# Layer 1 feed-forward entry: high parts of the first weights moved to ScalarE's gaps, modulation per channel tile, block sums on VectorE, one written order

## The chip, the cores and the metric

The kernel runs on one core of a Trainium2 chip. The metric is the device time of one execution in microseconds; three runs of the kernel before give a median of 1838.54 us (1838.1 to 1839.96). The engines are called by the names of the profile: PE is TensorE's matmuls, PEld its weight loads, DVE is VectorE, ACT is ScalarE, POOL is GpSimd, SP is SyncE, which here only issues transfers.

## The reference

The reference is one step of a two-layer trunk on 128 context tokens and 512 latent tokens of width 1024: layer 0 mixes tokens by differential attention, layer 1 by a bidirectional gated recurrence, and each layer ends with a dense SwiGLU feed-forward network. What matters here is where layer 1 enters its feed-forward network:

```python
def adanorm(x, g, shift, scale):
    return rmsnorm(x, g) * (1.0 + scale) + shift

def swiglu(h, w_in, w_out):
    gt, up = jnp.split(h @ w_in, 2, axis=-1)
    return (jax.nn.silu(gt) * up) @ w_out
...
        xs = xs + ms[2] * os_
        xs = xs + ms[5] * swiglu(adanorm(xs, g_norm_ffn[i], ms[3], ms[4]), w_ffn_in[i], w_ffn_out[i])
```

The hidden width is 2816. All inputs are fp32.

## The kernel before, in words

**Precision by parts.** Each operand of a product is split into a high part (an fp32r copy made by ACT) and a low part (source minus high part, made by DVE or POOL). A product is three matmuls: high by high, high by low, low by high. So nothing can be multiplied before an ACT copy and a subtraction have been made of it.

**Tokens and tiles.** The 640 tokens are five row tiles of 128 (t = 0 is the context). They are also two halves of 320, and the width of 1024 is eight channel tiles of 128 (k = 0 to 7). `Hf` holds the modulated activations in fp32, channels on partitions; `A1hi`/`A1lo` are the parts of the first half of the tokens, `A2hi`/`A2lo` and `S[:, 3]` those of the second half. `S` reuses the two tiles that held the attention-side operand `oT`, so it shows as `Thi`/`Tlo` in the profile.

**Entry to the feed-forward network, row tile by row tile.** The last product of the token mixer (`row_sums(t)`, 24 matmuls of 512 columns into `psr`) gives a row tile's second half. `close_rows(t)` adds it to the residual (two DVE steps), squares and sums it (ACT), makes the reciprocal root (three small POOL steps) and scales the rows (ACT) into an `xr` tile. `turn_rows(t)` transposes these rows on PE, eight blocks of 128 by 128, into two PSUM tiles `ntp` of four channel tiles each; there are only two such buffers, so the next row tile's transposes wait until this one's have been read. `modulate(t)` reads them: two DVE multiplications of 512 columns by the scale, broadcast along the tokens, and two additions of the shift, on POOL for t = 0, 1, 3 and on DVE for t = 2, 4. Then `hi_of` (ACT) and `lo_of` (DVE) make the parts.

**The first two hidden tiles, f = 0 and 1,** are multiplied in the plain way by `whole_in(ch, half)`: 48 matmuls of 320 columns each, SiLU on ACT and a product on DVE. Their weights `w0`, `w1` are two raw tiles each (`wr`, three buffers), split by `split_raw` (ACT 1024 columns, DVE 1024 columns) into `wh`, `wl` (six buffers each).

**From f = 2 on** `ffn_in` uses a seven-product block scheme (Strassen's with Winograd's sums) over the two halves of channels and tokens. It needs sums of activation blocks, made once by `sums(t)` for t = 2, 3, 4 (each two POOL steps, two DVE steps and the parts of three of the four results; the fourth, `s4`, is split by `put_late_sums`), and sums of weight blocks for each f, made by POOL in `ffn_weights(f)` (four steps) and split by ACT and DVE. The products are taken in the order 1, 2, 6, 5, 7, 3, 4; product 6 is added onto the PSUM tile of product 1 after ACT has copied it out.

**What sets the order.** A planner orders each engine's queue by its own cost estimates, with two exceptions. While `traced["order"]` is true, DVE, ACT and POOL instructions keep the order in which the code lists them; while `pe["strict"]` is true, the matmuls do. Weight loads on SP's queue (`load`) keep their order among themselves throughout. In the kernel before, both flags are cleared after `ffn_weights(2)`, ahead of the second `whole_in`. An instruction at the head of an engine's queue that waits holds up everything behind it.

## Time and profile before

| | |
|---|---|
| median of three runs | 1838.54 us (1838.1 to 1839.96) |
| profiled execution: time, span | 1841.69 us, 1839.9 us |
| PE busy | 1778.1 us, 97% of the span |
| DVE, ACT, POOL busy | 1219.6, 742.6, 663.8 us |
| stage of the change | about 1345 to 1445 us of the span |
| mean granted TensorE clock | 0.99 |

The profile comes from one execution, with its own time; the time lies 1.8 us above the span. Views by line all show line 51 for DVE, ACT and POOL and lines 96 and 99 for matmuls and transposes, since helpers record every operation, so instructions are told apart by the tiles that they write and read. A row of the timeline gives the start, the length, engine, line, operation, tiles, shape and count, and in brackets the idle time ahead of it and what ended it. "PEclk" is the granted clock as a share of full speed.

### The profile page before, as it was taken

The numbers are of one execution on the slowest core, as the hardware profiler recorded it, in microseconds if no ns is written. First come the engines' busy times: TensorE is split into PE (matmuls) and PEld (weight loads), VectorE is DVE, ScalarE is ACT, GpSimd is POOL, SyncE is SP. The second block draws the span as 40 slices with busy tenths as digits, with TensorE's granted clock in tenths as the row PEclk, the third lists the DMA queues.
The fourth block names the chain that finished last, engine by engine and source line by source line (L and its number), as shares of the span: only waits on it lengthen the run. The fifth ranks groups of instructions, "written<-read, shape, count | busy, mean of one in ns | idle before, by whom it ended". The sixth has DMA issues, their size and how long they took to land.

```text
span 1839.9 us, 34696 instructions
## 1 busy us (share of the span) xinstructions
PE 1778.1 (97%) x13791; PEld 1634.0 (89%) x13791; DVE 1219.6 (66%) x2092; ACT 742.6 (40%) x1642; POOL 663.8 (36%) x766
## 2 busy tenths in 40 slices
PE   6999999999999999999999999999998999999997
PEld 5799999878898999899799999999777898998896
DVE  4788888756266655855776777666658656566666
ACT  3566666635131122132353333333344443433443
POOL 3344544325000000000055455555324466466562
PEclk9999999999999999999999999999999999999999
DMA  9511221554364433453532222221222323233331
GB/s 316 175 44 44 64 66 38 167 183 121 92 200 136 148 115 121 154 145 115 155 118 64 65 65 62 62 64 65 70 89 65 102 87 114 81 98 109 92 104 69
DMA packets 222856, 195.27 MB, mean 106 GB/s; under 512 B 10276, under 2 KB 176606, under 8 KB 222694
## 3 DMA queue, kind: packets, MB, share of 16 engines
q1 hardware_dynamic: 221888, 192.46, 33.7%
q8 instruction: 108, 1.77, 0.4%
q10 hardware_dynamic: 806, 0.60, 0.1%
q14 instruction: 54, 0.44, 0.1%
HBM read 185.64 MB, written 7.37 MB: 105 GB/s over the span
## 4 chain that ended last, share of the span: by engine, by line
PE 82%; DVE 8%; DMA 4%; ACT 2%; issue 2%; POOL 2%; SPq 0%; POOLq 0%; ACTq 0%; DVEq 0%
PE psgu L96 22%; PE psr L96 19%; PE psqkv L96 8%; PE psf L96 8%; PE psvg L96 5%; PE psu L96 4%; PE pso L96 2%; PE S L96 2%; PE psg L96 2%; PE pa L96 2%; PE po L96 1%; DMA wr<-w_ada 1%; DVE Q L51 1%; PE ptp L99 1%; DVE wl L51 1%
## 5 line engine op out<-in xcount | busy, mean ns | idle before, releaser
L51 ACT ACTIVATE wh<-wr 128x1024 fp32r<-128x1024 f32 (+2 forms) x224 | 217.2, 976 | 385.1 <-DMA wr<-w_ffn_in 111.3
L51 DVE TENSOR_TENSOR wl<-wr,wh 128x1024 fp32r<-128x1024 f32 (+2 forms) x148 | 183.0, 1240 | 198.4 <-ACT wh L51 197.2
L96 PE MATMUL psgu<-Thi,wh 128*128 128x320 f32 x880 | 272.5, 311 | 2.7 <-ACT wh L51 2.6
L96 PE MATMUL psgu<-Tlo,wh 128*128 128x320 f32 x880 | 272.2, 309 | 1.2 <-DVE Tlo L51 1.2
L51 POOL TENSOR_TENSOR wl<-wr,wh 128x341 fp32r<-128x341 f32 (+2 forms) x228 | 212.5, 962 | 166.0 <-ACT wh L51 165.4
L96 PE MATMUL psgu<-Thi,wl 128*128 128x320 f32 x880 | 271.4, 310 | 0.9 <-DVE wl L51 0.9
L51 POOL TENSOR_TENSOR nss<-nss 128x1 f32<-128x1 f32 x24 | 7.5, 312 | 454.0 <-ACT xr L51 438.0
L96 PEld LDWEIGHTS psgu<-Thi,wh 128*128 128x128 f32 x880 | 165.5, 188 | 5.4 <-ACT wh L51 3.5
L96 PEld LDWEIGHTS psgu<-Tlo,wh 128*128 128x128 f32 x880 | 165.6, 188 | 2.3 <-DVE Tlo L51 1.4
L96 PEld LDWEIGHTS psgu<-Thi,wl 128*128 128x128 f32 x880 | 165.3, 188 | 2.3 <-DVE wl L51 1.8
L96 PE MATMUL psr<-wh,Thi 128*128 128x512 f32 x380 | 153.3, 405 | 0.5 <-ACT Thi L51 0.5
L96 PE MATMUL psr<-wh,Tlo 128*128 128x512 f32 x380 | 149.0, 392 | 0.0
L96 PE MATMUL psr<-wl,Thi 128*128 128x512 f32 x380 | 148.9, 392 | 0.0
L96 PE MATMUL psr<-wh,gT 128*128 128x512 f32 (+1 forms) x448 | 140.4, 388 | 1.0 <-DVE gT L51 0.6
L96 PE MATMUL psf<-Thi,wh 128*128 128x320 f32 x384 | 123.1, 321 | 0.0
L51 DVE SCALAR_TENSOR_TENSOR acc<-wr,cT,acc 128x512 f32<-128x512 f32 x168 | 116.1, 744 | 6.6 <-DMA wr<-w_ada 6.6
L96 PE MATMUL psf<-Thi,wl 128*128 128x320 f32 x384 | 118.5, 308 | 0.0
L96 PE MATMUL psf<-Tlo,wh 128*128 128x320 f32 x384 | 118.4, 308 | 0.0
L96 PE MATMUL psqkv<-wh,Thi 128*128 128x384 f32 x320 | 109.8, 359 | 1.0 <-ACT Thi L51 1.0
L96 PE MATMUL psqkv<-wh,Tlo 128*128 128x384 f32 x320 | 105.9, 345 | 0.5 <-DVE Tlo L51 0.5
L96 PE MATMUL psqkv<-wl,Thi 128*128 128x384 f32 x320 | 104.5, 342 | 0.0
L51 DVE TENSOR_TENSOR rtmp<-psr,gate 128x512 f32<-128x512 f32 (+1 forms) x101 | 66.2, 678 | 55.2 <-PE psr L96 45.9
(289 smaller groups left out, 4695.7 us busy)
## 6 DMA issues: line engine op xcount, KB each, us to landing
wr<-w_ffn_in SPq DMA_DIRECT2D x176, 256.0 KB
wr<-w_ada SPq DMA_DIRECT2D x72, 512.0 KB
wr<-w_ffn_out SPq DMA_DIRECT2D x40, 512.0 KB
wr<-w_in_rec SPq DMA_DIRECT2D x64, 256.0 KB
wr<-w_qkv_attn SPq DMA_DIRECT2D x64, 192.0 KB
ar<-w_ada SPq DMA_DIRECT2D x24, 512.0 KB
gate<-gdram SPq DMA_DIRECT2D x28, 256.0 KB
wr<-w_o_attn SPq DMA_DIRECT2D x8, 512.0 KB
```

The lines of the kernel that those rows point to most:

```text
L51: ins = op(*a, **k)
L96: in_order(nc.tensor.matmul(*a, **k))
L99: in_order(nc.tensor.transpose(*a, **k))
```

## The change

The change touches only layer 1's `out_and_ffn_1`.

1. **Modulation.** `modulate(t)` becomes eight DVE instructions of 128 columns, one per channel tile. Each multiplies by the scale and adds the shift in one step, both taken as one value per partition. The POOL and DVE additions go.
2. **High parts of `w0` and `w1`.** `split_raw` is taken apart into `whole_hi` (ACT) and `whole_lo` (DVE). The high parts of `w0` come right after `modulate(0)`; those of `w1` come in `close_rows(3)` between the sums of squares and the scaling of the rows (`hi_next`). The low parts follow after `modulate(1)` and after `modulate(3)`. The raw load of `w1` is listed right after `modulate(0)`, that of f = 2 (`raw2`) after `close_rows(4)`.
3. **Sums.** All four steps of `sums(t)` run on DVE; their parts become `put_sums(t)`, listed later. The weight sums of f = 2 run on DVE instead of POOL; those of later f stay on POOL.
4. **Order.** `turn_rows(3)` and `modulate(3)` move ahead of the low parts of row tile 2. The sums of row tiles 2, 3 and 4 are spread over the four `whole_in` calls, which are all listed ahead of the point where both flags are cleared: f = 0 and f = 1 on the first half of the tokens, then both on the second half. The four `put_gT` follow after `put_late_sums`, still in written order.

The diff, cut to its core:

```diff
-            def modulate(t, eng):
+            def modulate(t):
                 g = 0 if t == 0 else 1
-                has = [Hf[:, ks, t * P : (t + 1) * P] for ks in HALVES]
-                a, b = ([adaC[:, l, w, g, ks].unsqueeze(2).to_broadcast([P, 4, P]) for ks in HALVES] for w in (3, 2))
-                for ha, tp, c in zip(has, turned.pop(t), a):
-                    VE.tensor_tensor(ha, tp, c, ALU.mult)
-                for ha, c in zip(has, b):
-                    eng.tensor_tensor(ha, ha, c, ALU.add)
+                tps = turned.pop(t)
+                for k in range(KT):
+                    a, b = (adaC[:, l, w, g, k : k + 1] for w in (3, 2))
+                    VE.tensor_scalar(Hf[:, k, t * P : (t + 1) * P], tps[k // 4][:, k % 4], a, b, ALU.mult, ALU.add)
...
-                PO.tensor_tensor(a22, a21, a22, ALU.add)
+                VE.tensor_tensor(a22, a21, a22, ALU.add)
                 VE.tensor_tensor(a21, a11, a21, ALU.subtract)
                 VE.tensor_tensor(a11, a22, a11, ALU.subtract)
-                PO.tensor_tensor(s4, a12, a11, ALU.subtract)
+                VE.tensor_tensor(s4, a12, a11, ALU.subtract)
+                late_sums.append((c0, c1, s4))
+
+            def put_sums(t):
+                c0, c1 = max(t * P - HTOK, 0), (t + 1) * P - HTOK
                 split_rows([v[:, :, c0:c1] for v in S31], Hf[:, :, HTOK + c0 : HTOK + c1])
-                split_rows([v[:, 2, :, c0:c1] for v in S], a11)
-                late_sums.append((c0, c1, s4))
+                split_rows([v[:, 2, :, c0:c1] for v in S], Hf[:, 0:4, c0:c1])
...
+            def ffn_weights(f):
+                raw = raw_weights(f)
+                return all_weights(*plain_weights(raw), *weight_sums(raw, PO))
...
-            def close_rows(t, ps, xc, blocks=()):
+            def close_rows(t, ps, xc, between=lambda: None):
...
-                hi_of(blocks)
+                between()
                 unit_scale(sq, xs[t], xr[t])
...
+            def whole_hi(r):
+                hi = wp.tile([P, 1024], F32R, name="wh", tag="wh", bufs=6)
+                lo = wp.tile([P, 1024], F32R, name="wl", tag="wl", bufs=6)
+                AC.activation(hi, r, AF.Copy)
+                return r, hi, lo
+
+            def whole_lo(r, hi, lo):
+                VE.tensor_tensor(lo, r, hi, ALU.subtract)
+                return hi, lo
...
-            modulate(0, PO)
+            modulate(0)
+            w0 = [whole_hi(r) for r in w0]
+            w1 = whole_weights(1)
...
-            close_rows(2, ps2, xc, early_blocks(0))
+            close_rows(2, ps2, xc, lambda: hi_of(early_blocks(0)))
             xc = load_xc(3)
-            modulate(1, PO)
-            first[0].append(split_raw(w0[0], VE))
+            modulate(1)
+            hi_of(early_blocks(1))
+            first = [[whole_lo(*w) for w in w0]]
             lo_of(early_blocks(0))
-            hi_of(early_blocks(1))
             ps3, products = row_sums(3)
             drain(products)
-            close_rows(3, ps3, xc)
+
+            def hi_next():
+                w1[:] = [whole_hi(r) for r in w1]
+
+            close_rows(3, ps3, xc, hi_next)
             xc = load_xc(4)
-            first[0].append(split_raw(w0[1], VE))
-            w1 = whole_weights(1)
             lo_of(early_blocks(1))
             ps4, products = row_sums(4)
             take(products, 2)
             turn_rows(2)
-            modulate(2, VE)
+            modulate(2)
             hi_of(early_blocks(2))
             lo_of(early_blocks(2))
             drain(products)
-            close_rows(4, ps4, xc, late_blocks(2))
+            close_rows(4, ps4, xc, lambda: hi_of(late_blocks(2)))
+            raw2 = raw_weights(WHOLE)
+            turn_rows(3)
+            modulate(3)
             lo_of(late_blocks(2))
+            hi_of(late_blocks(3))
+            first.append([whole_lo(*w) for w in w1])
+            lo_of(late_blocks(3))
...
-                    turn_rows(3)
-                    modulate(3, PO)
-                    first.append([split_raw(w, VE) for w in w1])
-                    hi_of(late_blocks(3))
-                    lo_of(late_blocks(3))
+                    sums(2)
                     gus = [whole_in(first[0], 0)]
                     turn_rows(4)
-                    modulate(4, VE)
+                    modulate(4)
                     hi_of(late_blocks(4))
+                    put_sums(2)
                     lo_of(late_blocks(4))
-                    for t in range(2, NT):
-                        sums(t)
-                    weights = ffn_weights(WHOLE)
+                    sums(3)
+                    gus.append(whole_in(first[1], 0))
+                    put_sums(3)
+                    sums(4)
+                    h1, h2 = plain_weights(raw2)
+                    gus.append(whole_in(first[0], 1))
+                    put_sums(4)
+                    weights = all_weights(h1, h2, *weight_sums(raw2, VE))
+                    gus.append(whole_in(first[1], 1))
+                    open_group(nk)
+                    put_late_sums()
+                    for i, gu in enumerate(gus):
+                        put_gT(group, i % 2, i // 2, gu)
                     traced["order"] = False
                     pe["strict"] = False
-                    gus.append(whole_in(first[1], 0))
-                    open_group(nk)
-                    for f, gu in enumerate(gus):
-                        put_gT(group, f, 0, gu)
-                    for f in range(WHOLE):
-                        put_gT(group, f, 1, whole_in(first[f], 1))
```

`raw_weights`, `plain_weights`, `weight_sums` and `all_weights` are the four parts of the old `ffn_weights`, with the engine of the sums as an argument.

More of the change, by code (lines that the diff above doesn't have):

```diff
@@ L1626, in put_gT, with raw_weights, plain_weights, weight_sums @@
                 VE.tensor_tensor(gT[1][:, i, hs], v, gT[0][:, i, hs], ALU.subtract)
-            def ffn_weights(f):
+            def raw_weights(f):
                 cols = slice(f * P, (f + 1) * P)
-                r1, r2 = (load_raw(wi[:, 4 * c : 4 * c + 4, :, cols], [4, 2, P]) for c in range(2))
-                x1, x2 = (r.rearrange("p (k u c) -> p k u c", k=4, u=2) for r in (r1, r2))
-                b11, b12, b21, b22 = x1[:, :, 0], x1[:, :, 1], x2[:, :, 0], x2[:, :, 1]
-                h1 = split(b11, VE, [4, P])
-                h2 = split(x2, VE, [4, 2, P])
-                ta, tb = (xr_tile().rearrange("p (s k c) -> p s k c", s=2, k=4) for _ in range(2))
-                PO.tensor_tensor(ta[:, 0], b12, b11, ALU.subtract)
-                PO.tensor_tensor(ta[:, 1], b22, b12, ALU.subtract)
-                PO.tensor_tensor(tb[:, 0], b22, ta[:, 0], ALU.subtract)
-                PO.tensor_tensor(tb[:, 1], b21, tb[:, 0], ALU.subtract)
+                raw = [load_raw(wi[:, 4 * c : 4 * c + 4, :, cols], [4, 2, P]) for c in range(2)]
+                return [r.rearrange("p (k u c) -> p k u c", k=4, u=2) for r in raw]
+            def plain_weights(raw):
+                x1, x2 = raw
+                return split(x1[:, :, 0], VE, [4, P]), split(x2, VE, [4, 2, P])
+            def weight_sums(raw, eng):
+                b11, b12, b21, b22 = (x[:, :, u] for x in raw for u in range(2))
+                ta, tb = (xr_tile().rearrange("p (s k c) -> p s k c", s=2, k=4) for _ in range(2))
+                eng.tensor_tensor(ta[:, 0], b12, b11, ALU.subtract)
+                eng.tensor_tensor(ta[:, 1], b22, b12, ALU.subtract)
+                eng.tensor_tensor(tb[:, 0], b22, ta[:, 0], ALU.subtract)
+                eng.tensor_tensor(tb[:, 1], b21, tb[:, 0], ALU.subtract)
+                return ta, tb
+            def all_weights(h1, h2, ta, tb):
                 tb, ta = (
@@ L1661, in out_and_ffn_1, with ffn_in @@
             }
-            def ffn_in(f, w, group, i, between=lambda: None):
+            def ffn_in(w, group, i):
                 def product(ps, n, start):
@@ L1687, in ffn_in @@
                 AC.activation(b, sum1, AF.Copy)
-                between()
                 sum2 = mm_tile([P, HTOK], "psu")
@@ L1741, in whole_weights @@
                 return [load_raw(wi[:, 4 * c : 4 * c + 4, :, f * P : (f + 1) * P], [4, 2, P]) for c in range(2)]
+            def whole_hi(r):
[6 more added lines that the diff above has]
+                return hi, lo
             traced["order"] = True
             w0 = whole_weights(0)
-            first = [[]]
             for t in range(2):
@@ L1819, in out_and_ffn_1 @@
                 for f in range(max(f0, WHOLE), f1):
-                    if f == WHOLE:
-                        ffn_in(f, weights, group, f - f0, put_late_sums)
-                    else:
-                        ffn_in(f, ffn_weights(f), group, f - f0)
+                    ffn_in(weights if f == WHOLE else ffn_weights(f), group, f - f0)
                 gT = group["gT"]
```

## The prediction

> **What bounds the kernel now.** I read the busy times of the page first, then a table of stretches, then who waited for whom on PE, then the timelines of the engines around the waits. The first row is the whole span; the second is the sum row of a table over 1440 to 1840 us (width, then busy us).
>
> ```profile
> PE 1778.1 (97%) x13791; PEld 1634.0 (89%) x13791; DVE 1219.6 (66%) x2092; ACT 742.6 (40%) x1642; POOL 663.8 (36%) x766
> ...
> sum 400.00, PE 387.52 PEld 358.33 DVE 245.92 ACT 157.76 POOL 221.72; mean PE 32.29 PEld 29.86 DVE 20.49 ACT 13.15 POOL 18.48
> ```
>
> PE sets the time, and after 1440 us it is busy for 387.5 of 400 us, most of the rest being the last 15 us of stores. So time that PE wins at the feed-forward entry should travel to the end. The entry itself, by stretches (width; busy us of PE, PEld, DVE, ACT, POOL; granted clock; DMA share; GB/s):
>
> ```profile
> 1366.00:1381.00 15.00, 14.30 (x70) 11.21 (x68) 7.50 (x12) 8.91 (x19) 5.91 (x10) 1.00 0.12 36
> 1381.00:1396.00 15.00, 10.37 (x59) 10.20 (x60) 10.70 (x17) 8.39 (x16) 4.00 (x6) 0.77 0.12 37
> 1396.00:1418.00 22.00, 22.00 (x153) 21.85 (x151) 21.16 (x25) 10.21 (x18) 11.08 (x7) 1.00 0.25 73
> 1418.00:1430.00 12.00, 4.13 (x24) 3.50 (x24) 11.01 (x12) 4.60 (x10) 7.01 (x5) 0.90 0.29 87
> 1430.00:1434.20 4.20, 4.20 (x17) 4.20 (x18) 4.20 (x5) 2.21 (x5) 3.81 (x2) 0.50 0.04 14
> ...
> PE psu L96 <- ACT wh L51: 7.0, 1, 7.0
> PE ntp L99 <- DVE Hf L51: 5.3, 2, 5.1
> PE psgu L96 <- DVE wl L51: 0.6, 1, 0.6
> ```
>
> The last three rows are PE's waits from 1366 to 1435 us (total, times, longest). There are two holes, A at 1381 and B at 1418, and behind each the clock is down. PE's timeline at their edges, and a row of the chain of waits for twelve matmuls of 320 columns at full clock:
>
> ```profile
> 1380.14 0.40 PE L96 MATMUL psr<-wh,Tlo 128*128 128x512 f32 x1
> 1385.63 1.94 PE L99 MATMUL ntp<-ident,xr 128*128 128x128 f32 x8 [5.09 <-DVE Hf L51]
> 1387.22 0.61 PE L96 MATMUL psgu<-A1hi,wh 128*128 128x320 f32 x1
> ...
> 1389.97 0.31 PE L96 MATMUL psgu<-A1hi,wh 128*128 128x320 f32 x1
> ...
> 1418.74 0.42 PE L96 MATMUL psgu<-A1hi,wl 128*128 128x320 f32 x1 [0.62 <-DVE wl L51]
> ...
> 1420.97 0.42 PE L96 MATMUL psg<-A1hi,wl 128*128 128x320 f32 x1 [0.21 <-DVE wl L51]
> ...
> 1422.40 0.31 PE L96 MATMUL psg<-A1hi,wl 128*128 128x320 f32 x1
> 1429.74 0.64 PE L96 MATMUL psu<-Thi,wh 128*128 128x320 f32 x1 [7.03 <-ACT wh L51]
> ...
> 1434.17 0.39 PE L96 MATMUL psu<-Thi,wl 128*128 128x320 f32 x1
> ...
> 1443.58 1.76 PE psgu L96 x12
> ```
>
> One matmul is 1.76 / 12 = 0.147 us. Hole A loses 5.1 us idle. Then eight transposes take 1.59 us from start to start instead of about 0.8, and nine matmuls 2.75 us (1387.22 to 1389.97) instead of 1.3: 2.2 us to the low clock. Hole B loses, start to start, 7.34 - 0.15 = 7.2 us, about 1.2 us in the two short waits ahead of it, and 4.43 - 17 x 0.147 = 1.9 us to the low clock. Sum: 5.1 + 2.2 + 1.2 + 7.2 + 1.9 = **17.6 us**, the most that the change can win here.
>
> Why the holes are there:
>
> ```profile
> 1381.39 1.04 ACT L51 ACTIVATE wh<-wr 128x1024 fp32r<-128x1024 f32 x1
> ...
> 1382.46 1.22 DVE L51 TENSOR_TENSOR wl<-wr,wh 128x1024 fp32r<-128x1024 f32 x1 [4.28 <-ACT wh L51]
> 1384.81 1.28 DVE L51 TENSOR_TENSOR Hf<-ntp,adaC 128x512 f32<-128x512 f32 x2
> ...
> 1407.72 3.76 DVE L51 TENSOR_TENSOR Tlo<-Hf,Thi 128x1024 fp32r<-128x1024 f32 x2 [0.40 <-ACT Thi L51]
> ...
> 1420.84 4.51 DVE L51 TENSOR_TENSOR gT<-gu,gT 128x320 fp32r<-128x320 f32 x3
> ...
> 1427.70 1.99 ACT L51 ACTIVATE wh<-xr 128x1024 fp32r<-128x1024 f32 x2
> ...
> 1428.78 2.36 DVE L51 TENSOR_TENSOR wl<-xr,wh 128x1024 fp32r<-128x1024 f32 x2 [0.46 <-ACT wh L51]
> ...
> L51 POOL TENSOR_TENSOR xr<-wr 128x512 f32<-128x512 f32 x4 | 7.8, 1951 | 0.0
> ```
>
> A: DVE stands 4.28 us at the low part of the second `w0` tile, whose high part ACT makes only at 1381.39, after the rows of tile 3 are scaled. Queued behind it is the modulation of row tile 2 (1384.81), which must free the PSUM tiles for the transposes of row tile 3. B: DVE works without a break from 1396 on and puts `gT` parts ahead of what product 6 needs; the split of the weight sums starts on ACT at 1427.70. POOL, working alongside, makes DVE slower: two subtractions of 1024 columns take 3.76 us at 1407.72 and 2.36 us at 1428.78, and three of 320 columns take 4.51 us.
>
> **The change part by part.**
>
> *Modulation.* No row shows a two-scalar step out of PSUM. The nearest (form, count, durations in ns; for the second busy us and mean ns; then timeline rows):
>
> ```profile
> L51 DVE TENSOR_SCALAR F<-sg,omlb,lb x32: 437/454/1052, 942.1 to 1282.8; 128x320 f32<-128x320 f32 x32
> ...
> L51 DVE TENSOR_SCALAR orow<-o,rc,rs 128x128 f32<-128x128 f32 x40 | 14.2, 356 | 2.3 <-POOL rs L51 2.2
> ...
> 1347.74 1.39 DVE L51 SCALAR_TENSOR_TENSOR orow<-po,rs,gt 128x128 f32<-128x128 f32 x5 [4.99 <-POOL rs L51]
> ...
> 1365.92 1.28 DVE L51 TENSOR_TENSOR Hf<-ntp,adaC 128x512 f32<-128x512 f32 x2
> 1366.75 1.23 PE L99 MATMUL ntp<-ident,xr 128*128 128x128 f32 x8 [0.24 <-DVE Hf L51]
> ...
> L51 DVE TENSOR_TENSOR Hf<-ntp,adaC 128x512 f32<-128x512 f32 x10 | 6.4, 679 | 0.0
> ```
>
> Low bound: one scalar and a PSUM source, five in 1.39 us, about 0.26 us from start to start. High: with two scalars out of SBUF, 320 columns take 0.437 and 128 take about 0.34, so 0.5 ns per column and 0.27 us fixed; at the 1 ns per column of the 512-column rows (two in 1.28, one 0.68, so 0.60 each) a PSUM source gives 0.27 + 0.13 = 0.40 us. Instructions overlap by some 0.08 us (0.68 against 0.60), so I take **0.32 us** each, nearest to the second row, 2.6 us per row tile, with 0.26 and 0.40 as bounds. On DVE that replaces 1.2 us (t = 0, 1, 3) or 2.4 us (t = 2, 4).
>
> The Trainium skill, "VectorE: DVE Perf Modes", section "The TRN2 errata", speaks against this edit: a fixed cost falls on every instruction, and it advises tiles of at least 512 elements. Its formula from PSUM, (120 + 128) / 0.96 GHz, is an estimate of 0.26 us for each step, four of them 1.03 us against 0.66 us for one of 512; the trace's 0.68 us for 512 agrees, and the sum by it would be that of the low bound, 1824.3 us.
>
> The first row tile pays for it on PE. DVE reaches `modulate(0)` at 1365.92 as now; the first PSUM tile is free at 1365.92 + 3 x 0.32 + 0.40 = 1367.3, the second at 1368.6. Then four transposes (half of 1.23) end at 1369.2, against 1366.75 + 1.23 = 1368.0 now: **PE 1.2 us later** (0.8 and 2.0 at the bounds).
>
> *High parts.* ACT's waits that they are put into, and a row of the chain for 30 matmuls of 512 columns:
>
> ```profile
> 1370.16 0.63 ACT L51 ACTIVATE xr<-orow 128x512 f32<-128x512 f32 x1 [2.54 <-DVE orow L51]
> ...
> 1380.15 1.33 ACT L51 ACTIVATE xr<-orow,rs 128x512 f32<-128x512 f32 x2 [1.22 <-POOL rs L51]
> ...
> 1345.69 6.88 PE psr L96 x30
> ```
>
> The two of `w0` (0.95 us each, from 1.99 us for two) fall into the 2.54 us in which ACT waits for the residual step; they cost nothing, and 1.9 us of `close_rows(2)` if that cover were gone. `w0`'s low parts follow `modulate(1)` and nothing waits behind them for ACT any more. `w1`'s high parts stand between squares and scaling of row tile 3: 1.9 us on ACT, beside POOL's small steps, for which it waits 1.22 us now, so 0.7 us is added. Walking DVE and ACT: row sums 3 end 27 matmuls of 0.23 us after 1369.2, at 1375.4; DVE is through `modulate(1)`, two low parts of 1.14 and two of 0.6 at 1377.3, the residual steps end at 1378.7, the square at 1379.4, `w1`'s high parts at 1381.3, the scaled halves at 1381.9 and 1382.5. Row sums 4 end on PE at 1380.54 + 1.2 = 1381.7. `modulate(2)` frees its PSUM tiles at 1381.2 and 1382.4. So the transposes wait about 0.8 us, and the first whole product another 0.4 us for the low parts of row tile 2: **1.2 us where A lost 7.3**. The waits are short and the clock stays up, as behind the 0.62 us wait at 1418.74, where the next matmul started 0.25 us later.
>
> The second raw tile of `w1` is the tight one: its buffer comes free with the first low part of `w0`, at 1375.0. From issue to first use such a pair takes 4.6 us (last fence of this part), so it lands at 1379.6, 0.6 us before ACT wants it. Its `wh` buffer comes from a weight tile of row sums 4 whose last matmul ends at 1378.9.
>
> *Sums, parts and order, 1383.6 us on.* DVE's list until the weight sums of f = 2 are split: two residual steps 1.3; two modulations 5.1; low parts of row tiles 2 to 4 3.1 and of `w1` 2.3; sums 6.7 (four steps of 0.34 and eight of 0.6, with 0.1 more for each that needs the one before); their parts 4.4; three SiLU products 1.2; the raw weights' low parts 1.75; weight sums 2.6; their low parts 2.3. Together 30.8 us, and about 2.3 us of waiting for ACT and PE: DVE is done at 1416.7. POOL's share of this is now on DVE (about 6 us) but POOL is silent, so the 1024-column steps cost 1.14 and not 1.88. PE needs, from 1383.35, four whole products of 48 x 0.147 = 7.04, eight transposes 0.8, products 1 and 2 of f = 2 at 1.76 each: 1415.8. So DVE is the slower one by a little. I find two waits: the third whole product for the low part of row tile 4, **0.8 us**, and product 6, which needs ACT's copy of product 1 in a part tile that the last SiLU product frees at 1417.1: ready at 1418.6, **2.0 us**. B lost 10.3 us.
>
> Sum: 17.6 - (1.2 + 1.2 + 0.8 + 2.0) = **12.4 us**; 14.2 at 0.26 and 9.4 at 0.40. The profiled execution of 1841.69 us (span 1839.9 and 1.8 around it) would be 1829.3. The median of the runs lies 3.15 us below it, so **1838.54 - 12.4 = 1826.2 us**.
>
> What else is moved: `raw2` and the loads for f = 3 pass through three raw buffers on SP's queue. The second tile of f = 3 waits for `raw2`'s first buffer, free when DVE's second weight sum ends, about 1412; now it is issued at 1418.75.
>
> ```profile
> 1418.75 0.94 SPq L91 DMA_DIRECT2D wr<-w_ffn_in  x2
> ...
> 1443.57 0.92 SPq L91 DMA_DIRECT2D wr<-w_ffn_in  x2
> ...
> 1448.20 1.30 POOL L51 TENSOR_TENSOR xr<-wr 128x512 f32<-128x512 f32 x1 [5.74 <-DMA wr<-w_ffn_in]
> ```
>
> **The rivals.** *1. DVE becomes the bound.* Modulation at 0.40, and POOL's sums for f = 3 run beside the end of DVE's list, which then pays 1.5 times (3.76 against 2.36) on its last 2.7 us: 9.4 - 1.4 = 8.0, and 1.9 less if the wait before product 6, then 3.4 us, halves the clock, between 0.62 us, which did not, and 5.09, which did. Middle 7 us: 1831.5 us. For it: DVE's 21.16 of 22 us. Against: f = 3's second raw tile lands at 1416.6, so only one POOL step of 2 us can fall there. The Trainium skill, "TensorE: Matmul & The Clock Gate", section "What's actually happening", puts the drop at an idle window of about 3.4 us; both long holes agree, and by it the rival stands at the edge.
>
> *2. The loads carry the end.* f = 3's second raw tile comes only 1418.75 - 1412 = 6.7 us earlier; if PE then waits for f = 3, that is all: 1831.8 us. Against: its weight sums take four POOL steps of 2 us, done by about 1424, and PE wants them at 1431.
>
> *3. Slower: `w1`'s high parts block ACT.* They stand in ACT's fixed order ahead of the scaling of row tile 3; if the raw tile lands late, PE stops at its transposes, 1 us for 1 us beyond 0.6, and 2.2 us once for the clock. The gain is gone at 0.6 + 12.4 - 2.2 = 10.8 us of lateness, a load of 15 us instead of 4.6. At 15 us late it is 1838.54 - 12.4 + 2.2 + 14.4 = 1842.7 us. For it: the margin of 0.6 us; against: 36 GB/s in that stretch.
>
> *4. PE's matmuls after the flags are cleared are planned anew* and lose what was won: about 1838 us.
>
> **How the numbers follow.** The forecast has 0.65, rival 1 0.16, rival 2 0.11, rival 3 0.05, rival 4 0.03. 0.2% or 3.7 us is about what a measurement of this kernel can tell from no change; the first three cases are faster, so faster 0.92, same 0.03, slower 0.05. Range: down to 1821.0, the low bound of 1824.3 with product 6's wait filled by other matmuls and the first row tile's cost gone, up to 1833.0, which holds rivals 1 and 2.
>
> **What would show it.** Right: PE's wait at the transposes of row tile 3 under 1.5 us; clock 1.00 in every stretch from 1366 to 1434; forty modulation steps near 0.40 us each; DVE over 90% busy from 1384 to 1417 with POOL nearly idle; PE's longest wait ahead of product 6, about 2 us. Wrong: a modulation step off 0.34 to 0.48; ACT waiting at `wh<-wr` before row tile 3's scaling; a wait over 3.4 us and a stretch of clock 0.50; new waits of PE after 1430, above all for f = 3's parts.

## The result, and the profile after

The changed kernel takes **1825.84 us** (median of 4 runs, 1824.8 to 1827.52), the kernel before on the same chip 1838.35 us: ratio 0.9933 (95% interval 0.9921 to 0.9946). A second sample of the same kernel gave 1827.77 us (6 runs, 1823.89 to 1829.57) beside 1836.98 us: 0.9940 (0.9927 to 0.9954). The forecast was 1826.2 us, with 1821 to 1833 us as its range and "faster" at 0.92.

First, what the traces can be compared by. The same stretch of both, ahead of anything that the change touches (width; busy us of PE, PEld, DVE, ACT, POOL; granted clock; DMA share; GB/s), of the kernel before and then of the changed one:

```profile
0.00:120.00 120.00, 102.42 (x816) 85.86 (x817) 78.75 (x197) 61.28 (x158) 44.91 (x84) 0.94 0.62 203
```

```profile
0.00:120.00 120.00, 102.68 (x838) 86.33 (x839) 81.78 (x206) 63.49 (x164) 45.50 (x84) 1.00 0.63 205
```

The granted clock is 0.94 in one and 1.00 in the other, and the changed trace reaches the first modulation 5.91 us earlier (1360.01 against 1365.92 us) although every engine's list is the same up to there. The second trace of the changed kernel starts it at 1365.15 us. So that offset belongs to the execution. I therefore read each trace by its **stretch**: from the first modulation step on DVE to the end of the span. It was 1839.9 - 1365.92 = 473.98 us and is 1823.0 - 1360.01 = 462.99 us, in the second trace 1827.8 - 1365.15 = 462.65. The change wins **11.0 to 11.3 us**; 12.4 were forecast. The two traces differ by 0.34 us; I take less than 0.5 us for no difference.

How far the part behind the stage scatters can be read from all traces of this document, since every engine's list is the same there. The mark is the fourth gate load behind the stage, of the kernel before and then of the changed one:

```profile
1481.95 0.46 SPq L1498 DMA_DIRECT2D gate<-gdram  x1
```

```profile
1464.93 0.46 SPq L1498 DMA_DIRECT2D gate<-gdram  x1
```

From there to the end of the span thirteen of the fourteen traces take 357.9 to 358.3 us (357.95 and 358.07 in these two); the one of experiment 7's first kernel takes 358.9.

Where the time went, by stretches of the changed kernel:

```profile
1366.00:1381.00 15.00, 14.74 (x80) 12.33 (x79) 14.47 (x33) 10.79 (x24) 2.83 (x9) 1.00 0.25 70
1381.00:1396.00 15.00, 13.88 (x97) 13.61 (x97) 13.61 (x29) 6.63 (x12) 1.47 (x2) 1.00 0.36 107
1396.00:1418.00 22.00, 20.84 (x135) 19.53 (x134) 20.64 (x27) 13.06 (x22) 5.10 (x3) 1.00 0.16 48
1418.00:1430.00 12.00, 11.15 (x73) 10.97 (x74) 8.89 (x12) 5.63 (x9) 1.59 (x1) 1.00 0.44 148
1434.20:1823.00 388.80, 376.35 (x2210) 348.13 (x2208) 238.19 (x288) 153.18 (x266) 219.66 (x157) 0.99 0.31 94
```

Both holes are gone, the clock stands at 1.00 from 1366 to 1430 us, and from 1360 to 1435 us seven waits of PE of at most 1.14 us are left. Behind the stage PE is busy 376.35 of 388.80 us, 96.8%, as before (387.52 of 400). PE's timeline shows the seven waits in place:

```profile
1361.53 0.63 PE L99 MATMUL ntp<-ident,xr 128*128 128x128 f32 x4 [0.93 <-DVE Hf L51]
1362.80 0.63 PE L99 MATMUL ntp<-ident,xr 128*128 128x128 f32 x4 [0.65 <-DVE Hf L51]
1375.60 0.40 PE L96 MATMUL psr<-wh,Tlo 128*128 128x512 f32 x1
1376.26 1.27 PE L99 MATMUL ntp<-ident,xr 128*128 128x128 f32 x8 [0.26 <-ACT xr L51]
1377.28 0.39 PE L96 MATMUL psgu<-A1hi,wh 128*128 128x320 f32 x1
1377.64 0.41 PE L96 MATMUL psgu<-A1lo,wh 128*128 128x320 f32 x1
...
1393.97 0.41 PE L96 MATMUL psgu<-Tlo,wh 128*128 128x320 f32 x1 [1.12 <-DVE Tlo L51]
...
1412.22 0.41 PE L96 MATMUL psu<-Thi,wl 128*128 128x320 f32 x1 [0.26 <-DVE wl L51]
1414.99 0.41 PE L96 MATMUL psg<-A1hi,wh 128*128 128x320 f32 x1 [0.39 <-ACT wh L51]
1418.85 0.42 PE L96 MATMUL psgu<-A1hi,wl 128*128 128x320 f32 x1 [1.14 <-DVE wl L51]
```

The engines behind these waits, DVE first, then a row of ACT, three of POOL and two of SP's queue:

```profile
1360.01 2.64 DVE L51 TENSOR_SCALAR Hf<-ntp,adaC 128x128 f32<-128x128 f32 x8
...
1377.15 0.76 DVE L51 TENSOR_TENSOR A1lo<-Hf,A1hi 128x256 fp32r<-128x256 f32 x2 [0.46 <-ACT A1hi L51]
...
1391.83 2.09 DVE L51 TENSOR_TENSOR Tlo<-Hf,Thi 128x512 fp32r<-128x512 f32 x3 [1.22 <-ACT Thi L51]
...
1409.81 2.36 DVE L51 TENSOR_TENSOR wl<-xr,wh 128x1024 fp32r<-128x1024 f32 x2 [1.19 <-ACT wh L51]
...
1412.49 4.50 DVE L51 TENSOR_TENSOR Tlo<-s,Thi 128x256 fp32r<-128x256 f32 x3
1416.91 1.28 DVE L51 TENSOR_TENSOR gT<-gu,gT 128x320 fp32r<-128x320 f32 x3
1418.12 1.81 DVE L51 TENSOR_TENSOR wl<-wr,wh 128x512 fp32r<-128x512 f32 x2
```

```profile
1373.60 1.99 ACT L51 ACTIVATE wh<-wr 128x1024 fp32r<-128x1024 f32 x2
```

```profile
1391.14 1.30 POOL L51 TENSOR_TENSOR xr<-wr 128x512 f32<-128x512 f32 x1 [9.97 <-DMA wr<-w_ffn_in]
...
1411.26 2.06 POOL L51 TENSOR_TENSOR xr<-wr 128x512 f32<-128x512 f32 x1 [18.82 <-DMA wr<-w_ffn_in]
1413.29 3.15 POOL L51 TENSOR_TENSOR xr<-wr,xr 128x512 f32<-128x512 f32 x2
```

```profile
1407.36 0.93 SPq L91 DMA_DIRECT2D wr<-w_ffn_in  x2
...
1451.70 9.47 SPq L1498 DMA_DIRECT2D gate<-gdram  x3
```

What is to be seen: PE's last long wait, 1.14 us at 1418.85, is for the low part of f = 3's first weights (1418.12 on DVE). It stands behind the low parts of the late sums, which take 4.50 us at 1412.49 just while POOL makes f = 3's weight sums.

### The profile page after: what moved, and what is told of

Read it like the earlier page. It is cut to its first block, busy times and chain, and to the rows that moved or that the text cites. A ratio compares the mean times of both kernels' runs of the same rounds, so it can differ in the third digit from the quotient of the medians.

```text
span 1823.0 us, 34717 instructions
## 1 busy us (share of the span) xinstructions
PE 1770.5 (97%) x13791; PEld 1626.0 (89%) x13791; DVE 1219.6 (67%) x2128; ACT 742.0 (41%) x1642; POOL 643.0 (35%) x750
## 4 chain that ended last, share of the span: by engine, by line
PE 81%; DVE 9%; DMA 4%; issue 2%; ACT 2%; POOL 1%; SPq 0%; POOLq 0%; DVEq 0%; ACTq 0%
PE psgu L96 22%; PE psr L96 19%; PE psf L96 8%; PE psqkv L96 8%; PE psvg L96 5%; PE psu L96 4%; PE pso L96 2%; PE S L96 2%; PE psg L96 2%; PE pa L96 2%; PE po L96 1%; DMA wr<-w_ada 1%; DVE wl L51 1%; DMA ar<-w_ada 1%; DVE Q L51 1%
## 5 line engine op out<-in xcount | busy, mean ns | idle before, releaser
L51 DVE TENSOR_TENSOR wl<-wr,wh 128x1024 fp32r<-128x1024 f32 (+2 forms) x148 | 178.9, 1213 | 185.7 <-ACT wh L51 184.5
```

What stands on the lines that cost most here:

```text
L51: ins = op(*a, **k)
```

## The experiments

One kernel per row; "stretch" as above, from one trace each; the ratio is to the kernel before on the same chip. "Both of these" are the old modulation and the swapped low parts.

| kernel | median us | ratio (95%) | stretch us |
|---|---|---|---|
| before | 1838.35 | | 473.98 |
| changed | 1825.84 | 0.9933 (0.9921 to 0.9946) | 462.99 |
| changed, again | 1827.77 | 0.9940 (0.9927 to 0.9954) | 462.65 |
| before + early high parts of `w0` | 1832.76 | 0.9966 (0.9953 to 0.9980) | 467.49 |
| before + new modulation | 1840.77 | 1.0008 (0.9997 to 1.0019) | 475.69 |
| before + matmuls in hole A | 1839.95 | 1.0007 (0.9996 to 1.0018) | 473.97 |
| changed, sums on POOL | 1828.64 | 0.9937 (0.9916 to 0.9958) | 464.45 |
| changed, old modulation | 1828.58 | 0.9939 (0.9921 to 0.9958) | 463.07 |
| changed, low parts swapped | 1824.14 | 0.9926 (0.9912 to 0.9940) | 463.36 |
| changed, both of these | 1824.68 | 0.9934 (0.9919 to 0.9948) | 461.63 |
| changed, `w1` later | 1830.86 | 0.9951 (0.9935 to 0.9967) | 464.33 |
| changed, no weight sums for f = 3 | 1827.99 | 0.9938 (0.9924 to 0.9952) | 461.23 |
| both of these, f = 3 split early | 1827.30 | 0.9930 (0.9917 to 0.9942) | 461.57 |
| both of these, row tile 4 on ACT | 1823.96 | 0.9922 (0.9909 to 0.9936) | 459.18 |

The medians of kernels that differ by 1 or 2 us overlap; for these the stretch decides, and its own scatter is known from two traces of one kernel and from the part behind the stage only.

**1. Is the 5.9 us offset the program's?** The changed kernel unaltered.

> The changed kernel as it is, taken again. From the issue of the first residual tile (xc) of the stage to the first gate load behind it the trace of the kernel before has 122.6 us (1346.10 to 1468.71) and that of the changed one 111.5 us (1340.17 to 1451.70). If that stretch is a property of the program and the 5.9 us by which the two traces differ ahead of it belongs to the execution, this trace has 111.5 us again, within 0.5, whatever the time of its xc issue, and the median lies between 1824.5 and 1828.5 us. If the early 5.9 us belongs to the program, the xc issue is at 1340 us again.

Measured: first residual load of the stage at 1345.31 us, so the offset isn't the program's. The stretch to the gate load was 110.16 us and not 111.5 within 0.5: a miss. That load is a loose mark: here it is issued 14.32 us ahead of the fourth gate load and in the first trace 13.23 us, while the stretch to the end of the span agreed within 0.34 us. From here on I use the latter beside it.

**2. One part alone: early high parts of `w0`.**

```
             modulate(0, PO)
+            w0 = [whole_hi(r) for r in w0]
...
-            first[0].append(split_raw(w0[0], VE))
+            first[0].append(whole_lo(*w0[0]))
```

> The kernel before with one part of the change: both high parts of w0 directly behind the first modulation on ACT, the low parts where they were. By the prediction's steps hole A (5.1 us idle and 2.2 us of low clock) shrinks to about 1 us, since DVE no longer stands 4.28 us at the second low part; DVE's own list starts about 4 us earlier, so hole B keeps its 10.3 us and some 1 to 2 us more, because DVE and not PE sets its end. Sum: 5 us faster than before, about 1833.4 us. Rival 1, DVE carries nothing over and hole B grows by all that A loses: 1838 us. Rival 2, hole B doesn't grow at all: the full 6.3 us, 1832 us.

Measured: 5.6 us faster by the medians, 6.5 us by the stretch: 0.6 to 1.5 us more than my sum, next to rival 2. PE's waits in this kernel:

```profile
PE psgu L96 <- ACT wh L51: 4.0, 1, 4.0
PE psgu L96 <- DVE wl L51: 2.2, 1, 2.2
...
PE psg L96 <- DVE wl L51: 0.4, 1, 0.4
```

Hole A's wait for `Hf` is gone; hole B is left with 6.6 us of waits (4.0, 2.2, 0.4) where it had 7.9. So this one move is worth more than half of the change, and it isn't given back: the standing time that DVE saves at A reaches B. DVE comes to the `gT` parts 1412.20 - 1362.81 = 49.4 us behind its first modulation step, before 1420.84 - 1365.92 = 54.9 us:

```profile
1412.20 4.51 DVE L51 TENSOR_TENSOR gT<-gu,gT 128x320 fp32r<-128x320 f32 x3
```

**3. One part alone: the new modulation.**

```
-                for ha, tp, c in zip(has, turned.pop(t), a):
-                    VE.tensor_tensor(ha, tp, c, ALU.mult)
-                for ha, c in zip(has, b):
-                    eng.tensor_tensor(ha, ha, c, ALU.add)
+                for k in range(KT):
+                    a, b = (adaC[:, l, w, g, k : k + 1] for w in (3, 2))
+                    VE.tensor_scalar(Hf[:, k, t * P : (t + 1) * P], tps[k // 4][:, k % 4], a, b, ALU.mult, ALU.add)
```

> The kernel before with the new modulation alone (eight steps of 0.32 us instead of two of 0.6 us on DVE and two more on POOL or DVE). By the prediction's steps this part costs time: PSUM tiles of row tile 0 are freed 1.2 us later, those of row tile 2 behind hole A 1.3 us later, and DVE's list for hole B is 1.4 us longer for row tile 3. Together 2 to 4 us slower than before: 1840.5 to 1842.5 us, PE's wait at row tile 3's transposes above 5.09 us. The matmuls and splits behind the cleared flags are also planned in another order (the high parts of the weight sums of f = 2 ahead of the third high part of gT), which could give 1 us back. Rival: POOL's additions were slowing DVE down, and without them the kernel is 1 to 2 us faster: 1837 us.

Measured: 2.4 us slower by the medians, though with an interval that holds no change; 1.7 us slower by the stretch, a little below the 2 to 4 forecast. PE's waits at row tile 3's transposes and at hole B:

```profile
1382.34 1.09 PE L99 MATMUL ntp<-ident,xr 128*128 128x128 f32 x4 [5.74 <-DVE Hf L51]
...
1422.11 0.64 PE L96 MATMUL psu<-Thi,wh 128*128 128x320 f32 x1 [2.94 <-ACT wh L51]
```

5.74 us instead of 5.09, as expected; at hole B the wait is 2.94 us instead of 7.03, beside another of 1.62 us, so the new plan order can have given part back. But behind hole B the clock is down for longer, 10.3 us against 6.8 us (1427.5 to 1434.3) in the kernel before:

```profile
1422.00:1432.30 10.30, 8.53 (x29) 7.72 (x30) 9.88 (x11) 4.52 (x8) 3.79 (x2) 0.50 0.34 115
```

3.5 us more at half clock are up to 1.7 us of PE's time, as much as the whole difference. The edit wins nothing by itself; how much of the 1.7 us is DVE's longer work and how much the clock isn't shown.

**4. Does the low clock behind a hole cost what I put down?** 24 unused matmuls in hole A.

```
             drain(products)
+            again, products = row_sums(4)
+            drain(products)
             close_rows(4, ps4, xc, late_blocks(2))
```

> The kernel before with 24 more matmuls (a second product of row tile 4 whose result nothing uses) standing in hole A, so that PE isn't idle there. 24 of 0.23 us are 5.5 us, hole A is 5.1 us idle. If the low clock behind the hole is what cost 2.2 us, the transposes of row tile 3 and the nine matmuls behind them run at full clock and the kernel is about 1.5 us faster in the stretch from the first xc issue to the gate load, 121 us instead of 122.6, although it computes more; the granted clock between 1381 and 1396 us is near 1.00 instead of 0.77. If the transposes and matmuls were slow for another reason (their inputs), the time is the same or longer by the 0.4 us that the filling sticks out: 123 us.

Measured: 121.59 us to the first gate load, near the 121 forecast, but by the loose mark of experiment 1; to the end it is 473.97 us, the same as before. The granted clock from 1381 to 1396 us is 1.00. PE at that place:

```profile
1384.58 1.03 PE L99 MATMUL ntp<-ident,xr 128*128 128x128 f32 x8
1385.91 0.42 PE L96 MATMUL psgu<-A1hi,wh 128*128 128x320 f32 x1 [0.30 <-ACT A1hi L51]
...
1387.67 0.31 PE L96 MATMUL psgu<-A1hi,wh 128*128 128x320 f32 x1
...
1427.45 0.64 PE L96 MATMUL psgu<-Thi,wh 128*128 128x320 f32 x1 [5.22 <-ACT wh L51]
```

Nine matmuls take 1387.67 - 1385.91 = 1.76 us instead of 2.75: here the clock was the cause. From the transposes to the first matmul it is 1.33 us instead of 1.59, because PE now waits 0.30 us for `A1hi`, a wait that the low clock had hidden. So of my 2.2 us some 1.25 come back when PE stays warm, and even these are lost again at hole B (waits of 2.17, 0.51 and 5.22 us there). Time won on PE alone ahead of B was worth nothing here; time won on DVE in experiment 2 was.

**5. Order or engine: the sums on POOL again,** two of four per row tile and the weight sums of f = 2, order unchanged.

```
-                VE.tensor_tensor(a22, a21, a22, ALU.add)
+                PO.tensor_tensor(a22, a21, a22, ALU.add)
...
-                VE.tensor_tensor(s4, a12, a11, ALU.subtract)
+                PO.tensor_tensor(s4, a12, a11, ALU.subtract)
...
-                    weights = all_weights(h1, h2, *weight_sums(raw2, VE))
+                    weights = all_weights(h1, h2, *weight_sums(raw2, PO))
```

> The changed kernel with two of the four sums per row tile and the weight sums of f = 2 on POOL again, in the same fixed order. If the fixed order and the early high parts carry the gain of hole B, the time stays within 1.5 us of the changed kernel: 1825 to 1827.5 us. If taking POOL's work away carries it (POOL beside DVE stretches a subtraction of 1024 columns from 1.14 to 1.88 us, and a POOL step of 1024 columns in two halves takes 3.9 us), PE waits 4 to 6 us more ahead of the products of f = 2: 1830 to 1832 us.

Measured: stretch 464.45 us, 1.5 to 1.8 above the changed kernel, just outside the first theory and far from the 4 to 6 of the second. Moving the sums to DVE is the small part of hole B's gain. What POOL does to DVE is plain in DVE's timeline of this kernel:

```profile
1398.33 3.76 DVE L51 TENSOR_TENSOR Tlo<-Hf,Thi 128x1024 fp32r<-128x1024 f32 x2
...
1414.97 2.36 DVE L51 TENSOR_TENSOR wl<-xr,wh 128x1024 fp32r<-128x1024 f32 x2 [4.79 <-ACT wh L51]
```

3.76 us for the low parts that take 1.82 and 1.81 us in the changed kernel, and DVE then stands 4.79 us for high parts of weight sums that POOL is still making. PE waits 2.21 us at the hand-over and then runs at half clock:

```profile
1416.90:1420.20 3.30, 2.81 (x10) 2.81 (x11) 3.30 (x4) 3.30 (x8) 2.93 (x2) 0.50 0.01 2
```

So part of the 1.5 to 1.8 us is the clock behind that wait.

**6. The old modulation in the changed kernel** (additions on POOL for t = 0, 1, 3), as in the diff of 3 with the signs turned.

> The changed kernel with the old modulation (two multiplications of 512 columns on DVE, the two additions on POOL for row tiles 0, 1 and 3, on DVE for 2 and 4). By the trace of the changed kernel a row tile costs DVE 2.64 us now; here it costs 1.2 us for three of the five, and the transposes of row tile 1 get their PSUM tiles 1.4 us earlier. If that is all: 1.5 to 2.5 us faster than the changed kernel, about 1824 us. Rival: the additions on POOL, 1 us each and in the way of DVE, make the high parts that ACT takes from them later, and the time is the same or up to 2 us longer: 1826 to 1828 us.

Measured: 463.07 us by the stretch, no difference; a miss. Row tile 1's transposes came earlier (their waits fell from 1.58 to 0.25 us), but PE waited at the third whole product:

```profile
1397.98 0.41 PE L96 MATMUL psgu<-Tlo,wh 128*128 128x320 f32 x1 [2.18 <-DVE Tlo L51]
```

**7. The low part of row tile 4 first,** ahead of the parts of row tile 2's sums, in the changed kernel and in that of 6.

```
                     hi_of(late_blocks(4))
-                    put_sums(2)
                     lo_of(late_blocks(4))
+                    put_sums(2)
```

> The changed kernel with one swap: the low part of row tile 4 ahead of the low parts of row tile 2's sums on DVE. The third whole product waits 1.12 us for that low part now. If the order of these two is the cause, the wait falls below 0.3 us and the stretch from the first xc issue to the gate load is 111.5 - 1.2 = 110.3 us; the median can't tell it, 1824 to 1827 us. Rival: the low part itself waits for ACT (modulation of row tile 4 ends late), and the stretch stays at 111.5 us.

> The changed kernel with the old modulation (additions on POOL for row tiles 0, 1 and 3) and the low part of row tile 4 ahead of the low parts of row tile 2's sums. With the old modulation alone the stretch from the first xc issue to the gate load was 110.5 us, and its longest wait of PE, 2.18 us, stood at the third whole product. If the swap takes that wait away: 108.5 us, 3 us less than the changed kernel, median about 1823 us. If that time is given back at the hand-over to the products of f = 2, because DVE's low parts of the weight sums, at 1413.8 us there, come no earlier: 110.5 us, 1825 us.

Measured: in the changed kernel the wait for `Tlo` vanishes and the stretch doesn't move (463.36 us; to the gate load 109.94 us as forecast, but the second trace of the unswapped kernel has 110.16 there). PE's timeline has the waits at the hand-over to f = 2:

```profile
1412.77 0.41 PE L96 MATMUL psu<-Thi,wl 128*128 128x320 f32 x1 [0.88 <-DVE wl L51]
...
1419.39 0.41 PE L96 MATMUL psgu<-A1hi,wl 128*128 128x320 f32 x1 [1.15 <-DVE wl L51]
```

0.88 us where 0.26 stood: PE got there earlier and waited for the same low part, so half of the gain or more was lost again at the hand-over. A little of it is left in the stage: the fourth gate load comes 1465.68 - 1361.24 = 104.44 us behind the first modulation step, against 104.92 and 104.64 us in the two traces of the changed kernel. Behind the stage this trace has one wait that none of the others has at that place, which takes it away:

```profile
1564.74 0.41 PE L96 MATMUL psu<-Thi,wl 128*128 128x320 f32 x1 [0.76 <-DVE wl L51]
```

Whether that wait belongs to the swap or to the execution, one trace can't tell. With the old modulation as well, it is 461.63 us, 1.0 to 1.4 less, and 110.10 us to the first gate load: the second of the outcomes written down, not the 3 us hoped for. Against experiment 6 the same swap is worth 463.07 - 461.63 = 1.4 us, where a wait of 2.18 us and the low clock behind it went. The reading that fits is that DVE's list sets the hand-over as soon as PE's waits ahead of it are short; a long wait of PE still costs, because DVE's later steps need PE's products. This is argued from the timelines, not tested by itself.

**8. `w1`'s high parts out of `close_rows(3)`.**

```
-            close_rows(3, ps3, xc, hi_next)
+            close_rows(3, ps3, xc)
...
             hi_of(late_blocks(3))
+            hi_next()
             first.append([whole_lo(*w) for w in w1])
```

> The changed kernel with w1's two high parts out of the place between squares and scaling of row tile 3, and behind the high parts of row tile 3 instead. By the prediction's steps they cost 0.7 us where they stand; PE's wait at the transposes of row tile 3, 0.26 us in the trace of the changed kernel, and what it loses in front of the first whole product, 0.9 us together, fall to about 0.2 us, and the stretch from the first modulation step on DVE to the end of the span falls from 462.8 us by 0.7, or by nothing if DVE's list is what sets the hand-over anyway. Rival: in their new place they make w1's low parts late, which stand ahead of nothing but the sums, and DVE's list ends later: 463.5 us.

Measured: 464.33 us, 1.3 to 1.7 longer; a miss, and more than the rival's 463.5. The 0.7 us didn't come back either: the first whole product starts 1381.77 - 1364.57 = 17.20 us behind the first modulation step, in the changed kernel 17.27. DVE stood 2.10 us for the late high parts, and PE stood 2.68 us at the third whole product and ran at half clock behind it:

```profile
1388.79 2.36 DVE L51 TENSOR_TENSOR wl<-wr,wh 128x1024 fp32r<-128x1024 f32 x2 [2.10 <-ACT wh L51]
```

```profile
1399.60:1402.90 3.30, 2.98 (x11) 2.98 (x12) 3.20 (x6) 1.08 (x2) 0.00 (x0) 0.50 0.00 0
```

The place that rival 3 called dangerous is the better of the two: there the copies are made in time, and DVE doesn't stand for them.

**9. POOL's weight sums of f = 3 left out.**

```
-                return all_weights(*plain_weights(raw), *weight_sums(raw, PO))
+                if f == WHOLE + 1:
+                    sums = [x.rearrange("p k u c -> p (k u) c").rearrange("p (s k) c -> p s k c", s=2) for x in raw]
+                else:
+                    sums = weight_sums(raw, PO)
+                return all_weights(*plain_weights(raw), *sums)
```

> The changed kernel without POOL's four weight sums of f = 3: the products of f = 3 take the high and low parts of the raw weights in their place, so this part of the output is left out, and only the time is read. In the two traces of the changed kernel the three low parts of the late sums take DVE 4.5 us while POOL works on these sums, and PE's longest wait at the hand-over, 1.14 us, is for the low part of f = 3's first weights, which stands behind them in DVE's list. If POOL beside DVE is what stretches them (rival 1's mechanism, in a place that I did not name), the three take about 1.8 us, that wait is gone, and the stretch from the first modulation step on DVE to the end of the span, 463.0 and 462.6 us in the two traces of the changed kernel, is 461 to 461.8 us. If they are slow for another reason they take 4.5 us again; if PE waits for something else then, the stretch stays at 462.5 to 463 us although DVE is done earlier.

Measured: stretch 461.23 us, 1.4 to 1.8 less, and on DVE:

```profile
1417.16 1.62 DVE L51 TENSOR_TENSOR Tlo<-s,Thi 128x256 fp32r<-128x256 f32 x3
```

1.62 us instead of 4.50, in the same order. The wait for f = 3's low part falls from 1.14 and 1.16 to 0.42 us. POOL beside DVE was the cause, and it lay on the path. The Trainium skill, "SBUF — State Buffer", section "Who interferes with whom", says that a DVE instruction with two SBUF inputs contends with a GpSimd instruction that reads SBUF; this run agrees.

**10. f = 3's weights split ahead of the late sums,** on top of 7's second kernel.

```
                     open_group(nk)
+                    raw3 = raw_weights(WHOLE + 1)
+                    plain3 = plain_weights(raw3)
                     put_late_sums()
...
-                    ffn_in(weights if f == WHOLE else ffn_weights(f), group, f - f0)
+                    if f == WHOLE + 1:
+                        weights = all_weights(*plain3, *weight_sums(raw3, PO))
+                    ffn_in(weights if f <= WHOLE + 1 else ffn_weights(f), group, f - f0)
```

> The changed kernel with the old modulation, the low part of row tile 4 ahead of the low parts of row tile 2's sums (these two gave 461.6 us from the first modulation step on DVE to the end of the span, against 462.8), and the weights of f = 3 split ahead of the low parts of the late sums. PE's longest wait was 1.16 us for the low part of f = 3's first weights, which came at 1417.04 us behind the late sums; here it is ready 4 us earlier. If nothing else is late, 460.5 us, and a median of about 1823 us; if the late sums' low parts, now 2.5 us later, are waited for in their place: 461.5 to 462 us.

Measured: 461.57 us, nothing won: POOL's sums now stretch the weights' low parts (3.62 us for two), and PE waits 1.68 us for ACT's copy of a finished product instead, for which ACT has stood 1.48 us for DVE. That is the time of the second outcome written down, but not its wait.

**11. Less work on DVE: row tile 4 modulated on ACT,** on top of 7's second kernel, with row tile 3's sums ahead of row tile 4's low part.

```
+            def modulate_act(t):
+                tps = turned.pop(t)
+                for hf, block in enumerate(late_blocks(t)):
+                    for k in range(4 * hf, 4 * hf + 4):
+                        a, b = (adaC[:, l, w, 1, k : k + 1] for w in (3, 2))
+                        AC.activation(Hf[:, k, t * P : (t + 1) * P], tps[hf][:, k % 4], AF.Identity, bias=b, scale=a)
+                    hi_of([block])
...
-                    modulate(4)
-                    hi_of(late_blocks(4))
+                    modulate_act(4)
+                    sums(3)
                     lo_of(late_blocks(4))
                     put_sums(2)
-                    sums(3)
```

> The changed kernel with the old modulation for row tiles 0 to 3, and row tile 4 modulated on ACT (eight steps with scale and bias, ACT stands idle 3.82 us there in the trace of the kernel with the old modulation and the swapped low parts), with row tile 3's sums ahead of row tile 4's low part on DVE. DVE's list loses 3.5 us (1.28 and 2.18 us of row tile 4's modulation). If DVE's list sets the hand-over, as the equal stretches of the kernels that only moved a wait suggest (462.8 us as it was, 463.4 with the swap), PE's waits there (0.88, 0.39, 1.16 us) shrink by about 2 us: 459.5 us from the first modulation step on DVE to the end of the span against 461.6, about 3 us less than the changed kernel, median about 1823 us. Rival: eight steps on ACT take longer than DVE's two times two, and the third whole product waits for row tile 4's low part by 1 to 2 us: 461 to 463 us.

Measured: 459.18 us, 3.5 to 3.8 below the changed kernel; median 1823.96 us (1820.51 to 1825.1), ratio 0.9922. Each ACT step is short enough (four in 1.50 us), and of PE's waits only two are longer than 0.25 us (ACT's row, then the waits):

```profile
1385.79 1.50 ACT L51 ACTIVATE Hf<-ntp,adaC 128x128 f32<-128x128 f32 x4
```

```profile
PE psgu L96 <- DVE wl L51: 1.2, 1, 1.2
PE ntp L99 <- ACT xr L51: 0.5, 1, 0.5
```

Shortening DVE's list by 3.5 us, with the sums of row tile 3 moved in the same edit, moved the end by 2.45 us against 461.63. By the stretch this is the best version; by the medians it lies 1.9 us below the first sample of the changed kernel, which the intervals don't separate.

## Why the prediction was right, and which terms were off

**The time.** The direction and the mechanism were right: both holes closed, and the gain reached the end. From the fourth gate load to the end of the span both kernels take the same time, 357.95 and 358.07 us, so nothing was lost behind the stage (rival 4), and the 11.0 to 11.3 us won are far more than rival 2's 6.7. But 12.4 us was 1.1 to 1.4 too much (1838.54 - 12.4 is 1826.1, not the 1826.2 of the prediction). That the medians differ by 12.5 is luck: in the second sample they differ by 1836.98 - 1827.77 = 9.2.

**Term by term** (17.6 us to be won, 5.2 forecast as lost again):

- *Modulation.* 2.64 us per row tile, 0.32 us from start to start: as taken. The estimate of 0.26 us by the formula of the Trainium skill, "VectorE: DVE Perf Modes", section "The TRN2 errata", isn't what this trace shows: one step is 0.40 us long.
- *Row tile 1's transposes:* the second four end at 1362.80 + 0.63 = 1363.43, 3.42 us behind the first modulation step, before 2.06. So 1.4 us; forecast 1.2.
- *High parts and hole A.* `w1`'s copies start at 1373.60 without a wait; my walk had them at 1379.4, less 5.9 for the offset 1373.5. Rival 3 fell with that. PE loses 0.43 us from the last matmul of the row sums (1375.60 + 0.23) to the transposes, 0.2 in them (1.02 us for 0.8) and 0.2 at 1377.64: 0.9 us; forecast 1.2.
- *Third whole product:* 1.12 us of wait and a slow start, 1.3 us; forecast 0.8. In the second trace the wait was 0.67 us. The 0.8 us leave out that the list has the parts of row tile 2's sums in front of that low part, and that DVE waits 1.22 us for their high part. Experiment 7 shows that this term hardly counted: with the wait gone the stage is 0.2 to 0.5 us shorter, and the rest came back behind.
- *Hand-over:* **the mis-sized term.** Forecast: 2.0 us, one wait ahead of product 6. Measured: between 1412.22 and 1418.85 us 26 matmuls start in 6.63 us instead of 26 x 0.147 = 3.8, and 0.5 us is lost at both ends of that: 3.3 us, in waits of 0.26, 0.39 and 1.14 us and the slow starts around them. None of the three waits stands ahead of product 6: they stand in product 5 (`psu`) and twice in f = 3's first products, which the planner had mixed in. The step of the prediction that was wrong is where DVE's ledger ends. I ended it at the low parts of the weight sums (forecast 1416.7, that is 1410.8 with the offset; measured 1409.81 + 2.36 = 1412.2; the waits in it, 1.22 and 1.19 us, were 2.4 where I had 2.3, and the steps took some 1 us more than the 30.8). Behind them stand the late sums, the `gT` parts and f = 3's first low part, and PE needed the last of these.
- *Contention.* Rival 1 had POOL's sums beside the end of DVE's list, and I answered that only one POOL step of 2 us can fall there. This sentence was wrong: the load came about when I said (issued at 1407.36, forecast 1412 less 5.9, that is 1406.1), but my list ended too early, and 5.1 us of POOL's work fell beside the late sums. Its factor of 1.5 was too small as well: 3.76 against 2.36 us is 1.6, and the late sums' low parts took 2.8 times as long. Experiment 9 prices the contention at 1.4 to 1.8 us, as much as the 1.1 to 1.4 us by which the forecast missed. Rival 1's mechanism, DVE as the bound, was in part what happened, though its time of 1831.5 us was not: in experiment 4 and in the first kernel of 7 time won on PE ahead of the hand-over was worth 0 to 0.5 us, and in 2, 9 and 11 time won on DVE was worth 6.5, 1.4 to 1.8 and 2.45 us.

Sum of the losses by rows: 1.4 + 0.9 + 1.3 + 3.3 = 6.9, and 17.6 - 6.9 = 10.7 us, against 11.0 to 11.3 by the stretch. **Of the list of signs** the forty steps of 0.40 us, the clock, the short wait at row tile 3 and DVE's 91 and 94% in the two stretches held; "POOL nearly idle" did not (5.10 us in the third stretch), nor the wait ahead of product 6.

**What each part is worth.** The early high parts of `w0` alone 6.5 us; the sums on DVE 1.5 to 1.8; the new modulation -1.7 alone and nothing within the change. The rest, some 3 us, would be the fixed order with `w1`'s early parts: the kernels of experiments 2 and 5, which differ in these and in the modulation, lie 467.49 - 464.45 = 3.0 us apart. The order wasn't changed by itself.

## What to carry to other kernels

Find the engine whose list ends last at the hand-over between two stages, and cost an edit by what it does to that list: here 5.5 us more work for PE cost nothing, and a wait of PE of 1.12 us taken away was worth at most 0.5, while 3.5 us less on DVE were worth 2.5. A wait of PE of over 2 us is another matter, for the clock behind it. Here a copy that one engine makes for another was best put into an early gap of its maker (experiments 2 and 8). And a ledger must go on to the last item that the next stage's first products need, with a neighbour's work on the same memory priced beside it.

## What the runs showed of the hardware

**POOL beside DVE costs more than the 1.5 times that I put down.** Three low parts of 256, 512 and 512 columns take 1.62 us with POOL silent and 4.50 us while POOL subtracts from SBUF, 2.8 times as long; POOL's own step of 512 columns takes 2.06 us at 1411.26, where the one at 1391.14 in the same trace takes 1.30.

**A wait of 2.2 us can cost clock, and with a delay.** I had the point between 0.62 and 5.09 us. Behind waits of 2.17 us (early high parts alone) and 2.18 us (old modulation) PE runs on at full clock for 1.0 to 1.4 us and then for about 3 us at half. Stretches behind the first and then behind the second wait (granted clock is the third number from the end):

```profile
1410.00:1411.50 1.50, 1.41 (x9) 1.41 (x10) 1.50 (x2) 1.00 (x2) 1.50 (x2) 1.00 0.09 26
1411.50:1414.50 3.00, 2.62 (x11) 2.23 (x10) 3.00 (x3) 0.00 (x0) 3.00 (x2) 0.51 0.56 162
```

```profile
1398.00:1399.00 1.00, 1.00 (x7) 1.00 (x8) 1.00 (x2) 0.00 (x0) 0.00 (x0) 0.97 0.00 0
1399.00:1402.00 3.00, 3.00 (x13) 3.00 (x13) 2.90 (x6) 2.10 (x4) 0.00 (x0) 0.50 0.01 3
```

Behind 2.21 us (experiment 5) and 2.68 us (experiment 8) the clock was halved too, as shown there. Another wait of 2.17 us (experiment 4, at 1418.27) left the clock at 1.00, and so did the 1.68 us of experiment 10. The Trainium skill, "TensorE: Matmul & The Clock Gate", section "What's actually happening", has a window of 3.4 us that runs freely; a drop of about 3 us that comes or stays away with the same wait would agree with that, but a wait of 2.2 us is less than the idle window that it names. The 2.18 us wait of the old modulation was followed by 3 us at half clock, up to 1.5 us of PE's time that I had not priced. It may be part of why that kernel won nothing before the low parts were swapped; the wait and the clock went together, so the runs don't separate them.
